# Delta rule of a hybrid layer: block turns on VectorE in place of transfers through memory, decay masks from constants by accumulating transfers, and another order of the fill products

## Chip, cores and metric

One core of one Trainium2 chip runs one layer of a diffusion backbone. The metric is the device time of the whole kernel in microseconds, as the median of several runs. TensorE (PE), VectorE (DVE), ScalarE (ACT), GpSimd (POOL) and SyncE (SP, here only a queue of transfers) each work through their instructions in order; semaphores couple them.

## The reference, cut to what matters

The layer is: half a feed-forward block, then two mixers side by side (2-D neighbourhood attention, and a gated delta rule in both directions), merged by gates, then half a feed-forward block. The change lies in the delta rule. Per head, direction and chunk of 64 tokens (shortened; the last three lines stand for the scan's step):

```python
decay = jnp.exp(jnp.where(lower, g[..., :, None] - g[..., None, :], -jnp.inf))
m = jnp.where(strict, jnp.einsum('...ik,...jk->...ij', k_beta, k) * decay, 0.0)
uw = triangular_solve(jnp.eye(GDN_CHUNK) + m, rhs, left_side=True, lower=True, unit_diagonal=True)
# then a scan over the chunks:
v_new = u - w @ s
s_next = s * g_tot + k_tail^T @ v_new
o = q_decayed @ s + (q k^T * decay) @ v_new
```

The kernel uses steps of 128 tokens, and computes the inverse of I + m once per step rather than solving. There are six steps s (two over the context, four over the 512 latent tokens), four heads and two directions.

## The kernel before

**The stage.** All of this runs in one stage, from about 718 to 967 us of the profiled span. Two streams are woven into each other on TensorE.

*Fills.* The columns of w_in that the delta rule doesn't need (q, k, v of the attention, the gates) are computed meanwhile: `fill_spill` (L784) takes one column of 128 features, rounds its weights to a high part `wh` on ScalarE (CAST, L137) and takes the remainder `wl` on VectorE (L139), does 24 products of 128x512 (eight k, each high x high, high x low, low x high, by `mm3k`, L192 to L194), copies the result out on ScalarE and stores it. It yields after each quarter, six products. `turn(kind, i)` (L1064) is called at places of the delta rule; it adds `RATE[kind][i]` to an account and issues that many quarters, tied behind the last product of the delta rule. A scheduler with its own model of time then orders the instructions of each engine; TensorE takes them in that order.

*The delta rule.* Three bases bi, each of two steps s = 2 bi and 2 bi + 1, each step of two pairs of heads p; four 128x128 matrices (two directions, two heads) lie beside each other in a tile.
- `gram` (L1114), four times per base, makes the decay tile `Dt` (a row of cumulated gates broadcast to all partitions by a transfer from `gcd`, L1118; on VectorE subtract the column's gate and add the mask, four times, L1122; an exponential of 128x512 on ScalarE, L1123), the products k k^T and q k^T on TensorE (tiles `pq`; for s = 2, 3 they are copied to `kq` tiles, written to memory `kqd`, and read back for s = 4, 5, L1093 to L1098), then `Bt` (L1128) and `At` (L1134) on VectorE. `Bt` is written to memory `bd` (L1131). For s = 2 the decay lives in half of the output accumulators `oacc`, else in tiles `Dt`.
- `base_inverse` (L1140) inverts all 32x32 diagonal blocks of a base at once, on VectorE, row by row: 31 rows of a product and a reduction (L1159, L1160), with the blocks spread over the partitions. It reads the blocks from `bd` in pieces of 128 bytes into `Ltr` and `L` (L1152), turns half of them by a ScalarE copy (L1153), sets diagonals on GpSimd (L1146 to L1155), and writes the result `Xt` to memory `rd`.
- `inverse` (L1173), twice per base, reads four pieces of it into tiles T0 and T1 (L1180, all named T in the profile), transposes 32x32 blocks on VectorE (L1182, L1183) and then builds the 128x128 inverse from the blocks by small products (tiles `pi`), with VectorE (L1202, L1218, L1229), ScalarE (L1193, L1219, L1237) and GpSimd (L1194) between them.
- `scan_step` (L1249), once per step and pair, carries the state S: products `pc`, and on VectorE r, vn, S and the outputs.

The order in which these are written, each of them calling `turn`, is:

```python
step(grams(0)); base = grams(1); turn("l", 0)
inv_of(0, 0); step(base, 4); inv_of(0, 1); step(base)
scan_of(0, 0); scan_of(0, 1); base = grams(2); scan_of(0, 2); step(base, 2); scan_of(0, 3); step(base, 2)
inv_of(1, 0); step(base, 2); scan_of(1, 0); step(base)
scan_of(1, 1); inv_of(1, 1); inv_of(2, 0); scan_of(1, 2); scan_of(1, 3); inv_of(2, 1)
# then the four scans of base 2, gdn_out, and the attention (first product sc, L1446)
```

Of the kernel before, what the change touches and what calls it, by code (L numbers as in the profile page):

```python
# [58 lines left out]
def body(ctx, tc, I, out, dbg=None):  # L59
# [1054 lines left out]
    def gram(p, s, bd, g):  # L1114
# [3 lines left out]
        nc.sync.dma_start(Dt[:], bass.AP(gcd.tensor, gcd.offset + (4 * s + 2 * p) * P, [[0, P], [24 * P, 2], [1, 2 * P]]))  # L1118
        for m, (d, c, i) in enumerate(mats):
            msk = cst[:, (C_MF if d == 0 else C_MB):][:, 0:P]  # L1120
            with tc.issue_after(marks["At" if s > 3 else "Bt"]) if s > 1 else nullcontext():
                V.scalar_tensor_tensor(Dt[:, m], Dt[:, m], gcum[:, d, s, 2 * p + i:2 * p + i + 1], msk, op0=ALU.subtract, op1=ALU.add)  # L1122
# [17 lines left out]
    def base_inverse(bd, rd):  # L1140
# [6 lines left out]
        for q in range(4):  # L1147
            G.memset(Xt[32 * q:32 * q + 32].rearrange("p c k -> p (c k)")[:, q % 2:512:34], 1.0)
        st = 32 * P + 32
        for q in range(4):  # L1150
            dst = tr[32 * q:32 * q + 32] if q < 2 else L[32 * q:32 * q + 32]
# [1 line left out]
        S.copy(L[0:64].rearrange("p r c -> p c r"), tr[:])  # L1153

        G.memset(L[:].rearrange("p r c -> p (r c)")[:, 0:1024:33], -1.0)  # L1155
        for i in range(1, 32):
# [3 lines left out]
            V.tensor_reduce(Xt[:, 0:c, i], t[:, 0:c, 0:i + 1], AX, ALU.add, negate=True)  # L1160
# [12 lines left out]
    def inverse(bi, st, rd, Bts):  # L1173


        T0 = tl(gq, [P, 8, 32], "T0", 2)
# [5 lines left out]
        V.transpose(fl(T0, 0), fl(T1, 0))  # L1182
        V.transpose(fl(T1, 4), fl(T0, 4))  # L1183
# [7 lines left out]
        for b, r in enumerate(blk):  # L1191
            o = 32 * (b % 2)
            S.copy(T6[r, :, o:o + 32], T0[r])  # L1193
# [724 lines left out]
```

## Time and profile before

| | us |
|---|---|
| median of 3 runs | 1499.81 (1499.24 to 1501.12) |
| the profiled execution | 1495.44 |
| its span, first to last instruction | 1493.7 |
| TensorE busy in it | 1434.0 (96%), granted clock 0.993 on the mean |
| VectorE, ScalarE, GpSimd busy | 1144.7, 661.9, 212.4 |
| the delta-rule stage | 718 to 967 |

Times in the profile are microseconds from the start of the span. A row of the timeline has the start, the duration, the engine, the line, the operation, the tiles out<-in, the shape, and, in brackets, how long the engine had been idle and what released it. A row of the waits has the engine, what waited, what it waited for, then the total, the number of times and the longest. A row of groups has the count, the busy time, the mean of one in ns, and the idle time before. Matmuls overlap, so their durations are longer than the steps from one to the next.

### The profile page before, as it was taken

To read this page: it belongs to the slowest core of one execution; us is meant where nothing else is said; L and a number is where in the kernel's file an instruction comes from. 1 tells how busy PE (TensorE), PEld (TensorE's weight loads), DVE (VectorE), ACT (ScalarE), POOL (GpSimd) and SP (SyncE) were. 2 spreads that over 40 slices of the span, in tenths; PEclk is the share of its full clock that TensorE was granted. 3 is DMA by queue.
4 is the path that set the end of the run, shared out by engine and by line. 5 is a ranking of instruction groups with operands and counts; after the bars stand their busy time and mean duration, and the time that the engine had idled before them with its cause. 6 is when DMAs were issued, how large, how long until landed. Compare 5 with 4: busy or idle time off the path is not lost.

```text
span 1493.7 us, 23926 instructions
## 1 busy us (share of the span) xinstructions
PE 1434.0 (96%) x9117; PEld 1258.3 (84%) x9117; DVE 1144.7 (77%) x1975; ACT 661.9 (44%) x1090; POOL 212.4 (14%) x262
## 2 busy tenths in 40 slices
PE   6999999999999999999998899999999999999997
PEld 4778989999998777888886778877778999998886
...
GB/s 372 211 257 225 222 238 187 137 174 166 170 198 404 181 178 129 84 92 88 159 222 203 167 68 125 92 276 131 100 169 149 64 129 113 85 114 134 263 98 84
DMA packets 109236, 248.56 MB, mean 166 GB/s; under 512 B 29049, under 2 KB 44481, under 8 KB 109121
## 3 DMA queue, kind: packets, MB, share of 16 engines
...
## 4 chain that ended last, share of the span: by engine, by line
PE 71%; DMA 10%; DVE 9%; ACT 4%; issue 3%; POOL 1%; SPq 1%; DVEq 0%; ACTq 0%; POOLq 0%
PE ps L211 15%; PE pm L192 5%; PE pm L193 5%; PE pm L194 5%; PE ps L533 4%; PE ps L535 4%; PE ps L534 4%; PE ps L1692 3%; PE ps L1694 3%; PE ps L1693 3%; PE ps L193 3%; PE ps L192 3%; PE ps L194 3%; PE pc L1049 3%; DMA wr<-in_up_dram 2%
## 5 line engine op out<-in xcount | busy, mean ns | idle before, releaser
L139 DVE TENSOR_TENSOR wl<-wr,wh 128x1024 fp32r<-128x1024 f32 (+1 forms) x184 | 226.0, 1233 | 112.9 <-ACT wh L137 111.3
L137 ACT CAST wh<-wr 128x1024 fp32r<-128x1024 f32 (+1 forms) x184 | 185.6, 1013 | 278.5 <-PE pm L193 72.7
L192 PE MATMUL pm<-uxh,wh 128*128 128x512 f32 x320 | 131.6, 411 | 0.0
L194 PE MATMUL pm<-uxh,wl 128*128 128x512 f32 x320 | 126.3, 395 | 0.8 <-DVE wl L139 0.8
L193 PE MATMUL pm<-uxl,wh 128*128 128x512 f32 x320 | 126.5, 395 | 0.0
L211 PE MATMUL ps<-wh,hx 128*128 128x512 f32 x352 | 96.1, 391 | 0.1
L211 PEld LDWEIGHTS ps<-wh,hx 128*128 128x128 f32 x352 | 65.9, 188 | 14.5 <-ACT wh L137 0.5
L280 DVE SCALAR_TENSOR_TENSOR adap<-wr,crow 128x1024 f32<-128x1024 f32 x61 | 74.3, 1218 | 2.4 <-DMA wr<-in_w_adaT_dram 1.7
L192 PE MATMUL ps<-uh,wh 128*128 128x256 f32 (+1 forms) x208 | 69.2, 334 | 3.8 <-ACT wh L137 3.8
L194 PEld LDWEIGHTS pm<-uxh,wl 128*128 128x128 f32 x320 | 60.6, 190 | 13.8 <-DVE wl L139 0.9
L192 PEld LDWEIGHTS pm<-uxh,wh 128*128 128x128 f32 x320 | 60.8, 190 | 11.1 <-ACT spill L796 0.2
L193 PEld LDWEIGHTS pm<-uxl,wh 128*128 128x128 f32 x320 | 60.9, 190 | 10.3
L114 POOL TENSOR_TENSOR rs<-ve,mhalf 128x1 f32<-128x1 f32 (+2 forms) x46 | 49.0, 1066 | 140.6 <-DVE ve L110 138.2
L193 PE MATMUL ps<-ul,wh 128*128 128x256 f32 (+1 forms) x208 | 67.9, 327 | 0.0
L194 PE MATMUL ps<-uh,wl 128*128 128x256 f32 (+1 forms) x208 | 67.0, 328 | 0.0
L193 PE MATMUL ps<-uxl,wh 128*128 128x256 f32 (+1 forms) x192 | 60.5, 318 | 2.2 <-DVE uxl L139 2.2
L192 PE MATMUL ps<-uxh,wh 128*128 128x256 f32 (+1 forms) x192 | 59.8, 318 | 1.6 <-ACT uxh L137 1.4
L194 PE MATMUL ps<-uxh,wl 128*128 128x256 f32 (+1 forms) x192 | 60.1, 316 | 0.0
L137 ACT CAST wh<-ra 128x1024 fp32r<-128x1024 f32 x31 | 32.6, 1052 | 59.7 <-PE ps L534 20.2
L533 PE MATMUL ps<-ur,wh 128*128 128x384 f32 x168 | 56.5, 336 | 0.0
L534 PE MATMUL ps<-ur,wh 128*128 128x384 f32 x168 | 56.4, 336 | 0.0
L533 PE MATMUL ps<-uh,wh 128*128 128x384 f32 x168 | 56.4, 336 | 0.0
...
## 6 DMA issues: line engine op xcount, KB each, us to landing
...
```

Of the source, the lines that this page charges most:

```text
L114: G.tensor_tensor(rs[:], ve[:], mhalf[:, 0:n], ALU.pow)
L137: S.copy(hi, src)
L139: marks["lo"] = V.tensor_tensor(lo, src, hi.bitcast(F32), ALU.subtract).ins
L192: T.matmul(ps, a, uh[:, k, :], start=(k == 0), stop=False)
L193: T.matmul(ps, a, ul[:, k, :], start=False, stop=False)
L194: marks["mm"] = T.matmul(ps, b, uh[:, k, :], start=False, stop=(k == nk - 1)).ins
L211: T.matmul(banks[t][d][:, c0:c1], a[:, sl], b[:, d * 512 + c0:d * 512 + c1], start=first and j == 0, stop=last and j == 2)
L280: V.scalar_tensor_tensor(pr[:], raw[:], 1.0, crow, op0=ALU.mult, op1=ALU.mult, accum_out=col[:, c:c + 1])
L533: T.matmul(ps[:], a, mh, start=k == 0, stop=False)
L534: T.matmul(ps[:], a, ml, start=False, stop=False)
L535: T.matmul(ps[:], b, mh, start=False, stop=k == 3)
L1049: last[0] = T.matmul(*a, **k).ins
```

## The change

It does six things.
1. The order of the 24 products of a fill: first, for each k, high x high and high x low (16 products), then all eight with the low part of the weights. They stand on one line now (L790).
2. Other numbers in `RATE`.
3. The decay tiles of s > 1: a constant mask `msk` is brought by a transfer on SP, the row of gates is added to it by an accumulating transfer that GpSimd issues, and ScalarE takes four exponentials of 128x128 with the column's negated gate (`ngc`) as the bias. The VectorE operations of L1122 and the single exponential stay for s < 2 alone. For s = 3 the tile is one of the `r` tiles.
4. The diagonal blocks of `Bt` are copied by ScalarE into a compact tile `W`, four copies per `gram` (`blocks`), and turned into `L` by two transpositions on VectorE, the second of 1024 columns with a strided source; `bd`, `Ltr` and their transfers go. The diagonal is set on VectorE.
5. The start values of `Xt` come from a constant `xt0` by a transfer.
6. `Xt` is turned to `Z` on VectorE, copied to T0 and T1 by four ScalarE copies, and transposed as before; `rd` and its transfers go. `inverse` takes the finished tiles.

```diff
         px = tl(pm, [P, NX], *PMB)
-        for k in range(KT):
-            if k and k % (KT // parts) == 0:
+        prods = [(w[0], u, k) for k in range(KT) for u in (uxh, uxl)] + [(w[1], uxh, k) for k in range(KT)]
+        for n, (a, u, k) in enumerate(prods):
+            if n and n % (3 * KT // parts) == 0:
                 yield
-            mm3k(px[:], w[0], w[1], uxh, uxl, k)
+            marks["mm"] = T.matmul(px[:], a[:, k * P:k * P + P], u[:, k, :], start=n == 0, stop=n == 3 * KT - 1).ins
...
-    RATE = {"g": (2, 3.0, 0.7), "l": (7.2,), "i": (1.5, 0, 0), "s": (0.7, 0.9, 0.5)}
+    RATE = {"g": (2, 2.4, 0.6), "l": (2,), "i": (1.2, 0.2, 0.7), "s": (0.6, 0.8, 0.9)}
...
+    ngc = tl(gq, [P, 2, 6, 4], "ngc")
+    S.activation(ngc[:], gcum[:], AF.Copy, scale=-1.0)
...
+        if s == 3:
+            return tl(gq, [P, 4, P], "r", 2)[:]
         return tl(gb_, [P, 4, P], "Dt", 2)[:]
...
+    def blocks(W, Bt, p, st):
+
+        m0 = 4 * st + p
+        for b in range(4):
+            r = slice(32 * b, 32 * b + 32)
+            marks["W"] = S.copy(W[r, 8:24].rearrange("p (d m) c -> p d m c", d=2)[:, :, m0:m0 + 3:2], Bt[r, :, r].rearrange("p (d i) c -> p d i c", d=2)).ins
+
+    def gram(p, s, W):
...
+        row = bass.AP(gcd.tensor, gcd.offset + (4 * s + 2 * p) * P, [[0, P], [24 * P, 2], [1, 2 * P]])
+        if s > 1:
+            nc.sync.dma_start(Dt[:], I["msk"])
+            with tc.issue_after(marks["Tt"]) if s > 4 else nullcontext():
+                G.dma_start(Dt[:], row, accum_op=ALU.add)
+        else:
+            nc.sync.dma_start(Dt[:], row)
         for m, (d, c, i) in enumerate(mats):
-            msk = cst[:, (C_MF if d == 0 else C_MB):][:, 0:P]
-            with tc.issue_after(marks["At" if s > 3 else "Bt"]) if s > 1 else nullcontext():
+            if s > 1:
+                with tc.issue_after(marks["Ti" if s > 4 else "Wg"]):
+                    S.activation(Dt[:, m], Dt[:, m], AF.Exp, bias=ngc[:, d, s, 2 * p + i:2 * p + i + 1])
+            else:
+                msk = cst[:, (C_MF if d == 0 else C_MB):][:, 0:P]
                 V.scalar_tensor_tensor(Dt[:, m], Dt[:, m], gcum[:, d, s, 2 * p + i:2 * p + i + 1], msk, op0=ALU.subtract, op1=ALU.add)
-        S.activation(Dt[:], Dt[:], AF.Exp)
+        if s < 2:
+            S.activation(Dt[:], Dt[:], AF.Exp)
...
-                nc.sync.dma_start(bass.AP(bd.tensor, bd.offset + g * MSTR, [[P, P], [4 * MSTR, 4], [1, P]]), Bt[:])
+                blocks(W, Bt, p, s % 2)
...
-        tr = tl(gb_, [64, 32, 32], "Ltr")
-        Xt = tl(gb_, [P, 16, 32], "Xt", 2)
-        G.memset(Xt[:], 0.0)
...
-            nc.sync.dma_start(dst, bass.AP(bd.tensor, bd.offset + (q // 2) * 8 * MSTR, [[st, 32], [P, 32], [1, 32]]))
-        S.copy(L[0:64].rearrange("p r c -> p c r"), tr[:])
-
-        G.memset(L[:].rearrange("p r c -> p (r c)")[:, 0:1024:33], -1.0)
+        with tc.issue_after(marks["Z"]) if "Z" in marks else nullcontext():
+            V.transpose(W[:, 0:8].rearrange("p m c -> p (m c)"), W[:, 16:24].rearrange("p m c -> p (m c)"))
+        V.transpose(L[:].rearrange("p r c -> p (r c)"), W[:, 0:16].rearrange("p m c -> p c m")[:, :, None].to_broadcast([P, 32, 2, 16]))
+        V.memset(L[:].rearrange("p r c -> p (r c)")[:, 0:1024:33], -1.0)
...
-        nc.sync.dma_start(bass.AP(rd.tensor, rd.offset, [[512, P], [1, 512]]), Xt[:].rearrange("p c k -> p (c k)"))
+        Z = tl(gb_, [P, 16, 32], "bt")
+        marks["Z"] = V.transpose(Z[:].rearrange("p c k -> p (c k)"), Xt[:].rearrange("p c k -> p (c k)")).ins
+        z = Z[:].rearrange("p c (q m) -> p m (c q)", q=2)
+        fl = lambda t, m: t[:, m:m + 4].rearrange("p m c -> p (m c)")
+        for st in range(2):
+            T0 = tl(gq, [P, 8, 32], "T0", 2)
+            T1 = tl(gq, [P, 8, 32], "T1", 2)
+            S.copy(T0[:, 0:4], z[:, 4 * st + 8:4 * st + 12])
+            S.copy(T1[:, 4:8], z[:, 4 * st:4 * st + 4])
+            V.transpose(fl(T1, 0), fl(T0, 0))
+            V.transpose(fl(T0, 4), fl(T1, 4))
+            turned.append((T0, T1))
         yield
...
-    def inverse(bi, st, rd, Bts):
-
-
-        T0 = tl(gq, [P, 8, 32], "T0", 2)
-        T1 = tl(gq, [P, 8, 32], "T1", 2)
-        for dst, d in ((T1, 0), (T0, 1)):
-            for q in range(2):
-                nc.sync.dma_start(dst[q:P:2, 4 * d:4 * d + 4], bass.AP(rd.tensor, rd.offset + (2 * d + q) * 16384 + st * 2048, [[32, 64], [2 * 2048, 4], [1, 32]]))
...
+    def inverse(bi, st, Bts):
+
+        T0, T1 = turned.pop(0)
...
+        marks["Wg"] = marks.get("W")
+        W = tl(gb_, [P, 24, 32], "W")
+        Xt = tl(gb_, [P, 16, 32], "Xt", 2)
+        nc.sync.dma_start(Xt[:].rearrange("p c k -> p (c k)"), I["xt0"])
...
+    a["xt0"] = _start()
+    a["msk"] = np.repeat(a["cst"][:, C_MF:C_MF + 2 * P].reshape(P, 2, 1, P), 2, 2).reshape(P, 4, P)
```

The change moves instructions on the engines; three places.

TensorE around the first product of base 2's first inverse (`pi<-T,Bt`). Before, the scan's products (`pc`) stand among fill products (`pm`):

```order
4350 L193 MATMUL pm_9053<-uxl_4691,wh_8979 128x512
4351 L194 MATMUL pm_9053<-uxh_4690,wl_8980 128x512
4352 L1049 MATMUL pc_9083<-vn_9076,ktail_9078 128x128 x4
4353 L1049 MATMUL pc_9093<-S_1619_8724,qT_5227 128x128
4354 L1049 MATMUL pc_9093<-S_1619_8724,qT_5228 128x128
4355 L1049 MATMUL pc_9093<-S_1619_8724,qT_5227 128x128
4356 L1049 MATMUL pc_9093<-S_1619_8724,qT_5228 128x128
4357 L192 MATMUL pm_9053<-uxh_4690,wh_8979 128x512
4358 L1049 MATMUL pi_8870<-T_1632_8854,Bt_8139 32x32 x4
4359 L1049 MATMUL pi_8870<-T_1632_8854,Bt_8166 32x32 x4
4360 L1049 MATMUL pi_8870<-T_1632_8854,Bt_8139 32x32 x4
4361 L1049 MATMUL pi_8870<-T_1632_8854,Bt_8166 32x32 x4
```

After, the lines of TensorE ahead of that inverse:

```order
4080 L1051 MATMUL pc_8943<-vn_8910,At_7453 128x128 x4
4081 L1051 MATMUL pc_8963<-S_1603_8626,kT_5223 128x128
4082 L1051 MATMUL pc_8963<-S_1603_8626,kT_5224 128x128
4083 L1051 MATMUL pc_8963<-S_1603_8626,kT_5223 128x128
4084 L1051 MATMUL pc_8963<-S_1603_8626,kT_5224 128x128
4085 L1051 MATMUL pc_8979<-r_8974,Tt_1278_6937 128x128 x4
4086 L1051 MATMUL pc_8997<-vn_8990,ktail_8992 128x128 x4
4087 L1051 MATMUL pc_9007<-S_1603_8626,qT_5227 128x128
4088 L1051 MATMUL pc_9007<-S_1603_8626,qT_5228 128x128
4089 L1051 MATMUL pc_9007<-S_1603_8626,qT_5227 128x128
4090 L1051 MATMUL pc_9007<-S_1603_8626,qT_5228 128x128
4091 L1051 MATMUL pi_8766<-T_1580_8534,Bt_8034 32x32 x4
```

The fill products have left this place: from the row of the inverse before it (the last `pi<-Tt,Y`) to this one there is now no fill among the scans of steps (1, 2) and (1, 3). Counted over the stage, 515 fill products stand ahead of this inverse before, and 388 now; behind it 107 and 234. Ahead of the very first `pi` product of base 0 there were 256 and are 196, and ahead of the last `pq` product 30 fewer.

VectorE where base 0 begins. Before, the masks of the next grams and two weight remainders stand between the last `Bt` and the first row:

```order
815 L1128 SCALAR_TENSOR_TENSOR Bt_7059<-pq_7043,beta_5207,oacc_1279_6940 128x128 x4
816 L1122 SCALAR_TENSOR_TENSOR oacc_1278_6939<-oacc_1278_6939,gcum_5208,cst_5205 128x128 x4
817 L1122 SCALAR_TENSOR_TENSOR oacc_1279_6940<-oacc_1279_6940,gcum_5208,cst_5205 128x128 x4
818 L1122 SCALAR_TENSOR_TENSOR Dt_7405<-Dt_7405,gcum_5208,cst_5205 128x128 x4
819 L139 TENSOR_TENSOR wl_7102<-wr_7099,wh_7101 128x1024
820 L1122 SCALAR_TENSOR_TENSOR Dt_7489<-Dt_7489,gcum_5208,cst_5205 128x128 x4
821 L139 TENSOR_TENSOR wl_7266<-wr_7263,wh_7265 128x1024
822 L1159 TENSOR_TENSOR bt_7147<-L_7133,Xt_7135 128x2
823 L1160 TENSOR_REDUCE Xt_7135<-bt_7147 128x1
```

After, in their place:

```order
815 L1149 SCALAR_TENSOR_TENSOR Bt_7071<-pq_7052,beta_5207,oacc_1280_6942 128x128 x4
816 L138 TENSOR_TENSOR wl_7117<-wr_7114,wh_7116 128x1024
817 L1165 STREAM_TRANSPOSE W_7005<-W_7005 128x256
818 L1166 STREAM_TRANSPOSE L_7148<-W_7005 128x1024
819 L1167 MEMSET L_7148 128x32
820 L1171 TENSOR_TENSOR bt_7152<-L_7148,Xt_7006 128x2
821 L1172 TENSOR_REDUCE Xt_7006<-bt_7152 128x1
```

The masks (L1122) are gone, and the transpositions of W and L and the diagonal stand ahead of the first row. One of the two weight remainders has moved into the rows (`wl_7288`, behind nine of them).

VectorE at the end of base 0. Before:

```order
896 L1159 TENSOR_TENSOR bt_7234<-L_7133,Xt_7135 128x15x31
897 L1160 TENSOR_REDUCE Xt_7135<-bt_7234 128x15
898 L1159 TENSOR_TENSOR bt_7237<-L_7133,Xt_7135 128x512
899 L1160 TENSOR_REDUCE Xt_7135<-bt_7237 128x16
900 L139 TENSOR_TENSOR wl_7572<-wr_7569,wh_7571 128x1024
901 L1122 SCALAR_TENSOR_TENSOR Dt_8159<-Dt_8159,gcum_5208,cst_5205 128x128 x4
902 L1159 TENSOR_TENSOR bt_7803<-L_7789,Xt_7791 128x2
```

After:

```order
894 L1171 TENSOR_TENSOR bt_7242<-L_7148,Xt_7006 128x512
895 L138 TENSOR_TENSOR wl_7569<-wr_7566,wh_7568 128x1024
896 L1172 TENSOR_REDUCE Xt_7006<-bt_7242 128x16
897 L1153 TENSOR_TENSOR At_8058<-kq_8055,Dt_8027 128x512
898 L1176 STREAM_TRANSPOSE bt_7245<-Xt_7006 128x512
899 L1165 STREAM_TRANSPOSE W_7259<-W_7259 128x256
900 L1166 STREAM_TRANSPOSE L_7716<-W_7259 128x1024
901 L1184 STREAM_TRANSPOSE T_1342_7248<-T_1341_7247 128x128
902 L1185 STREAM_TRANSPOSE T_1341_7247<-T_1342_7248 128x128
903 L1184 STREAM_TRANSPOSE T_1344_7254<-T_1343_7253 128x128
904 L1185 STREAM_TRANSPOSE T_1343_7253<-T_1344_7254 128x128
```

An `At` product of s = 4 on a `kq` tile read back from memory stands ahead of the transposition to Z (named `bt` here, since it takes a buffer of that tile); behind it stand the next base's W and L and the transpositions of T. On ScalarE, sixteen of the new exponentials (for the two `oacc` halves and the two `r` tiles) stand between base 0's last copies to W and the rounding `wh_7287`, whose remainder is `wl_7288`; eight more (of `Dt`) stand ahead of the last copy to a `kq` tile.

More of the change, by code (lines that the diff above doesn't have):

```diff
@@ L31 @@
 BWD_CH = (1, 0, 5, 4, 3, 2)
-MSTR = P * P + P
 C_MF = 0
@@ L1137, in gram, with base_inverse @@
         return Bt, At
-    def base_inverse(bd, rd):
+    turned = []
+    def base_inverse(W, Xt):
         L = tl(gb_, [P, 32, 32], "L")
-        tr = tl(gb_, [64, 32, 32], "Ltr")
-        Xt = tl(gb_, [P, 16, 32], "Xt", 2)
-        G.memset(Xt[:], 0.0)
[L1147 to L1151, printed above, removed]
-            nc.sync.dma_start(dst, bass.AP(bd.tensor, bd.offset + (q // 2) * 8 * MSTR, [[st, 32], [P, 32], [1, 32]]))
-        S.copy(L[0:64].rearrange("p r c -> p c r"), tr[:])
-        G.memset(L[:].rearrange("p r c -> p (r c)")[:, 0:1024:33], -1.0)
+        with tc.issue_after(marks["Z"]) if "Z" in marks else nullcontext():
+            V.transpose(W[:, 0:8].rearrange("p m c -> p (m c)"), W[:, 16:24].rearrange("p m c -> p (m c)"))
+        V.transpose(L[:].rearrange("p r c -> p (r c)"), W[:, 0:16].rearrange("p m c -> p c m")[:, :, None].to_broadcast([P, 32, 2, 16]))
+        V.memset(L[:].rearrange("p r c -> p (r c)")[:, 0:1024:33], -1.0)
         for i in range(1, 32):
@@ L1159, in base_inverse @@
             V.tensor_tensor(t[:, 0:c, 0:i + 1], L[:, i:i + 1, 0:i + 1].to_broadcast([P, c, i + 1]), Xt[:, 0:c, 0:i + 1], ALU.mult)
-            V.tensor_reduce(Xt[:, 0:c, i], t[:, 0:c, 0:i + 1], AX, ALU.add, negate=True)
+            marks[("row", i)] = V.tensor_reduce(Xt[:, 0:c, i], t[:, 0:c, 0:i + 1], AX, ALU.add, negate=True).ins
             if i % 4 == 0:
                 yield
-        nc.sync.dma_start(bass.AP(rd.tensor, rd.offset, [[512, P], [1, 512]]), Xt[:].rearrange("p c k -> p (c k)"))
+        Z = tl(gb_, [P, 16, 32], "bt")
[10 more added lines that the diff above has]
+            turned.append((T0, T1))
         yield
@@ L1193, in inverse @@
             S.copy(T6[r, :, o:o + 32], T0[r])
-            G.tensor_copy(Tt[r, :, 32 * b:32 * b + 32], T1[r])
+            marks["Tt"] = G.tensor_copy(Tt[r, :, 32 * b:32 * b + 32], T1[r]).ins
         py = tl(pgq, [P, 4, 32], "pi", 2)
@@ L1236, in inverse @@
         for b in range(2):
-            S.activation(Tt[hb[1 - b], sysm(b), hb[b]], p1[hb[1 - b]], AF.Copy, scale=-1.0)
+            marks["Ti"] = S.activation(Tt[hb[1 - b], sysm(b), hb[b]], p1[hb[1 - b]], AF.Copy, scale=-1.0).ins
         return [[Tt[:, 4 * d + 2 * i + p] for d in range(2) for i in range(2)] for p in range(2)]
@@ L1324, in body @@
     Sst = [None, None]
-    res, rds, inv = {}, {}, {}
+    res, inv = {}, {}
     def grams(bi):
-        bd = tl(dp, [16 * MSTR], f"bd{bi}")[:]
-        rds[bi] = tl(dp, [64, 1024], f"rd{bi}")[:]
+        marks["Wg"] = marks.get("W")
+        W = tl(gb_, [P, 24, 32], "W")
+        Xt = tl(gb_, [P, 16, 32], "Xt", 2)
+        nc.sync.dma_start(Xt[:].rearrange("p c k -> p (c k)"), I["xt0"])
         for j in (0, 2, 1, 3) if bi == 0 else range(4):
-            res[(bi, j)] = gram(j % 2, 2 * bi + j // 2, bd, 2 * (j % 2) + j // 2)
-        return base_inverse(bd, rds[bi])
+            res[(bi, j)] = gram(j % 2, 2 * bi + j // 2, W)
+        return base_inverse(W, Xt)
     def step(gen, n=8):
@@ L1338, in inv_of @@
     def inv_of(bi, st):
-        inv[(bi, 2 * st)], inv[(bi, 2 * st + 1)] = inverse(bi, st, rds[bi], [res[(bi, 2 * st + p)][0] for p in range(2)])
+        inv[(bi, 2 * st)], inv[(bi, 2 * st + 1)] = inverse(bi, st, [res[(bi, 2 * st + p)][0] for p in range(2)])
     def scan_of(bi, j):
@@ L1833, in _consts, with _start @@
     return c
+def _start():
+    t = np.zeros((P, 16, 32), np.float32)
+    for q in range(2):
+        for c in range(16):
+            t[np.arange(P) % 32 // 16 == q, c, 2 * c + q] = 1.0
+    return t.reshape(P, 512)
 def _rope():
```

9 lines of the change are left out of this document (1 added, 8 removed).

## The prediction

> **What bounds the kernel now.** I read the page first, then the stage that the change touches, from 718 us to the first attention product, by windows of 20 us and as a whole, then what TensorE waits for there, then the places in the timelines of TensorE and VectorE. The page's row of engines, and three windows (length, then busy time and instructions of PE, PEld, DVE, ACT and POOL, the granted clock, the DMA share, GB/s):
>
> ```profile
> PE 1434.0 (96%) x9117; PEld 1258.3 (84%) x9117; DVE 1144.7 (77%) x1975; ACT 661.9 (44%) x1090; POOL 212.4 (14%) x262
> ```
> ```profile
> 820.00:840.00 20.00, 16.65 (x170) 13.72 (x169) 16.83 (x42) 7.34 (x17) 0.00 (x0) 1.00 0.60 198
> 718.00:967.00 249.00, 231.67 (x1938) 194.65 (x1936) 186.41 (x492) 102.69 (x200) 36.30 (x69) 0.99 0.50 151
> 913.50:967.00 53.50, 50.21 (x534) 43.11 (x533) 31.00 (x68) 18.16 (x41) 14.26 (x21) 1.00 0.23 76
> ```
>
> TensorE is idle for 249.00 - 231.67 = 17.3 us of the stage, 14.0 of them ahead of 913.5 and 3.3 behind. That is all an edit here can win while TensorE's own work stays. What it waits for, in the stage and in its last part:
>
> ```profile
> PE pi L1049 <- DVE Y L1229: 5.1, 3, 2.4
> PE pi L1049 <- DMA T<-rd: 4.3, 1, 4.3
> PE pi L1049 <- DVE T L1218: 1.6, 2, 1.0
> PE pq L1049 <- DVE Xt L1160: 0.9, 1, 0.9
> PE pm L194 <- DVE wl L139: 0.8, 1, 0.8
> ```
>
> Only 4.3 us wait for a transfer by name; most of the rest waits for VectorE, busy 16.83 of 20 us at 820. TensorE's fill products follow each other every 0.2265 us (a mean over undisturbed stretches; the first two rows below are such a pair), and the engine stands still until the first product on the inverses:
>
> ```profile
> 797.05 0.39 PE L193 MATMUL pm<-uxl,wh 128*128 128x512 f32 x1
> 797.28 0.39 PE L194 MATMUL pm<-uxh,wl 128*128 128x512 f32 x1
> 802.00 0.92 PE L1049 MATMUL pi<-T,Bt 32*32 32x32 f32 x32 [4.33 <-DMA T<-rd]
> 913.49 0.45 PE L1049 MATMUL pi<-T,Bt 32*32 32x32 f32 x32
> 966.99 0.39 PE L1446 MATMUL sc<-kah,qah 64*128 64x256 f32 x2
> ```
>
> On VectorE the places are the end of base 0's products, the first row of its inverse, its last row, and the last row of base 2:
>
> ```profile
> 743.55 2.18 DVE L1122 SCALAR_TENSOR_TENSOR oacc<-oacc,gcum,cst 128x128 f32<-128x128 f32 x8
> 755.99 0.16 DVE L1159 TENSOR_TENSOR bt<-L,Xt 128x2 f32<-128x2 f32 x1 [5.03 <-POOL L L1155]
> 790.12 0.69 DVE L1160 TENSOR_REDUCE Xt<-bt 128x16 f32<-128x512 f32 x1
> 900.62 0.68 DVE L1160 TENSOR_REDUCE Xt<-bt 128x16 f32<-128x512 f32 x1
> ```
>
> **The change, part by part.** The whole transport of the blocks goes. From 743.55 to 756.0 the rows of base 0 now wait 12.4 us for it. The durations for the new steps, from the stage's groups:
>
> ```profile
> L1122 DVE SCALAR_TENSOR_TENSOR Dt<-Dt,gcum,cst 128x128 f32<-128x128 f32 x32 | 10.0, 377 | 7.8 <-DMA Dt<-gcd 7.8
> L139 DVE TENSOR_TENSOR wl<-wr,wh 128x1024 fp32r<-128x1024 f32 x27 | 33.0, 1222 | 3.5 <-ACT wh L137 2.0 <-PE pi L1049 1.5
> L1182 DVE STREAM_TRANSPOSE T<-T 128x128 f32<-128x128 f32 x6 | 1.8, 303 | 3.5 <-DMA T<-rd 3.5
> L1153 ACT COPY L<-Ltr 64x1024 f32<-64x1024 f32 x3 | 6.3, 2111 | 3.3 <-DMA Ltr<-bd 3.3
> L1193 ACT COPY T<-T 32x256 f32<-32x256 f32 x24 | 9.7, 402 | 8.3 <-issue 4.3 <-DVE T L1182 3.2 <-DMA T<-rd 0.6
> L1219 ACT ACTIVATE Tt<-pi 32x128 f32<-32x128 f32 x24 | 6.4, 268 | 4.8 <-PE pi L1049 4.5
> ```
>
> In its place: the last two sets of W copies on ScalarE behind a weight rounding, about 2.7 us (eight pieces at 0.268, the nearest row, 2.1, and what is queued); the turn of W, 0.4; the turn of L, 1024 columns with a strided source, bounded by 1.22 (a contiguous pass of 1024 on VectorE) and 2.11 (ScalarE's strided copy), taken at 1.7. So base 0 starts at 743.55 + 2.7 + 0.4 + 1.7 = 748.4, 7.6 us earlier. All 48 W copies cost ScalarE 48 x 0.268 = 12.9 us against 6.3 for the copies removed; it is busy 102.69 of 249, so I cost the total at nothing, but not its queue (below).
>
> These 7.6 us aren't the gain. VectorE does rows, products, scans and weight remainders one after another from there to base 2's end, now 145.3 us, in which it waits:
>
> ```profile
> DVE Dt L1122 <- DMA Dt<-gcd: 7.0, 2, 3.9
> DVE bt L1159 <- POOL L L1155: 6.4, 2, 5.0
> DVE T L1182 <- DMA T<-rd: 2.1, 2, 1.7
> DVE At L1134 <- DMA kq<-kqd: 1.8, 2, 1.1
> DVE T L1183 <- DMA T<-rd: 1.6, 1, 1.6
> DVE vn L1269 <- PE pc L1049: 1.5, 2, 1.2
> ```
>
> Those inside the stretch (5.0 of the L wait lies ahead of it) come to 7.0 + 1.4 + 2.1 + 1.8 + 1.6 + 1.5 and four small ones of 2.5: 17.9, so work and issue take 127.4. The masks removed give back 16 of 32 in this stretch (the others lie ahead), at 0.28 from start to start (8 took 2.18) 4.5 us; three weight remainders move behind the stretch, 3 x 1.22 = 3.7. Against that, eight more scan operations fall into it, 8 x 0.28 = 2.2, and the turns: L twice 3.4, W twice 0.8, Z three times (512 columns, between 0.30 and 1.22, taken at 0.6) 1.8, memsets 0.4. Sum 127.4 - 8.2 + 8.6 = about 128: VectorE's work here stays the same. What goes is waiting: the masks' 7.0, the block tile's 1.4, the T transfers' 3.7; 5.8 stay. Base 2 ends at 748.4 + 128 + 5.8 = 882.2, and its T is ready after Z, two copies of 0.40 and two turns of 0.30 at 884.2, against 913.5.
>
> TensorE can't follow. In the order it has 388 fill products ahead of that inverse instead of 515 and 234 behind it instead of 107. Without any wait it would be there at 913.5 - 14.0 - 127 x 0.2265 = 870.7, so it waits some 13.5 us for VectorE, about the 14.0 of now, in other places: at the first pi product (60 fills fewer ahead: TensorE there at 797.67 - 13.6 - 1.7 = 782.4; T at 748.4, plus the rows' 34.8 us of now, an At product of 0.6 and 3 for Z, W, L and T, 786.8: 4.4 us, as large as now), and in the scan products that stand without any fill ahead of base 2's inverse. From 884.2 the rest is now's 53.5 plus 127 x 0.2265 = 28.8, 966.5, less the waits of the tail, now 3.3, of which I let 2.7 go because twice the fills stand there. The stage ends at 963.8 instead of 967.0: **3.2 us** less. The reordered fill products are the same 24 per column; they hide the low part's arrival, 0.8 us of wait above, in those waits already.
>
> The clock. Now two windows show a lower granted clock:
>
> ```profile
> 802.00:806.00 4.00, 3.94 (x70) 2.73 (x70) 2.40 (x12) 2.18 (x5) 1.57 (x4) 0.57 0.70 168
> 866.00:870.00 4.00, 1.78 (x35) 1.28 (x33) 3.81 (x16) 1.71 (x5) 0.49 (x2) 1.00 0.00 0
> 870.00:874.00 4.00, 3.53 (x50) 3.16 (x46) 2.71 (x9) 0.76 (x2) 0.00 (x0) 0.57 0.02 4
> ```
>
> One follows the gap of 4.33, one a window in which TensorE was busy 1.78 of 4 us in pieces. Such a window loses at most 4 x 0.43 = 1.7 us. I keep two drops, as now (the first pi product and the bare scan chain), so nothing in the sum. The Trainium skill ("TensorE: Matmul & The Clock Gate", Part 1) gives an idle window of about 3.4 us for the drop to half; the first row agrees, the second shows that short gaps close together do it too. By its rule the bare scan chain, with short waits only, would not drop, and the sum would be 1.7 us better, -4.9; by the row it drops there as well.
>
> Moved queues. SP loses the block, L and T transfers and gains masks and start values, all early. GpSimd loses its memsets and issues eight accumulating transfers. Times from issue to landing, for row transfers, the kq round trip and GpSimd's own accumulating transfers elsewhere in the kernel:
>
> ```profile
> Dt<-gcd SPq DMA_DIRECT2D x8, 256.0 KB, 5.6
> kqd<-kq SPq DMA_DIRECT2D x8, 256.0 KB, 4.1
> kq<-kqd SPq DMA_DIRECT2D x16, 128.0 KB, 3.3
> L590 POOL DMA_DIRECT2D accd<-hx x6: 531/531/597, 207.1 to 243.3; - x6
> DMA to landing us min/median/max: 2.9/4.5/8.8
> ```
>
> **Rivals.** *More than the waits named go* (A). If the remaining 5.8 us of VectorE's waits vanish too, because its partner TensorE has fewer fills ahead of each scan product, T of base 2 is ready at 878.4 and the stage ends at 958.0, 9 us less: -6 to -10. For it: five waits on TensorE's products stand in that stretch. Against: these are short, and the kq waits are transfers.
>
> *The time moves into another wait, no change* (B). Ahead of base 0's turn of Z the order puts an At product on a kq tile read back from memory; its buffer is free once the last kq copy is written out. The last such product now:
>
> ```profile
> 783.00 1.05 PE L1049 MATMUL pq<-qT,kT 128*128 128x128 f32 x8
> ```
>
> With 30 fills fewer ahead it ends at 784.05 - 30 x 0.2265 - 1.7 = 775.6; ScalarE reaches the copy behind eight exponentials (8 x 0.32, estimated from 0.268) and a spill near 780, and 4.1 + 3.3 later it is 787.4, where VectorE is at 748.4 + 35.4 = 783.8: 3.6 us of stall, the gap at the first pi becomes 8, and the stage ends where it does now: -1 to +2.
>
> *Slower, by ScalarE's queue* (C). Sixteen exponentials stand there ahead of the rounding of the second weight column, and VectorE's remainder of that column stands nine rows into base 0. They wait for mask (landed 738.8, if issued at 733.3 where the row transfers now go, plus 5.5), then the accumulating rows, four issues of 0.53 and a landing of 4.5 to 8.8: 745 to 750. ScalarE needs the last of them at about 750. From about 752 on, each microsecond stops VectorE's rows one for one, with fills, pi products and scans behind it: landing at 758 makes 6 us, less the 3.2, and twice such (the second base has the same pattern) makes +4 to +8. The Trainium skill ("SBUF — State Buffer", the box on the "DVE blocks DMA" trap) speaks for this: descriptors of a transfer issued by GpSimd wait while VectorE holds the shared port; by it such landings come late when VectorE is busiest. The rows above (2.9 to 8.8 with VectorE at work) show a spread that may be this, but no stall past 8.8.
>
> *The change doesn't do what it says* (D): the order shows the transfers and masks gone, so this is only a slip of the scheduler elsewhere, either sign.
>
> **How the numbers follow.** The profiled execution took 1495.44 (span 1493.7), 4.4 under the median 1499.81; I carry the difference over: 1499.8 - 3.2 = 1496.6. About 0.2% (3.0 us) is what a measurement here can tell from no change, so my forecast lies at that border. Chances: forecast (-1.5 to -5.5) 0.45, of which 0.27 is over the border; A 0.18; B 0.19, of it 0.15 within and 0.04 slower; C 0.14; D 0.04 slower. Faster 0.45, same 0.33, slower 0.22. The range takes A to its end and C to its beginning: 1489.5 to 1504.0.
>
> **What would show it.** Right: base 0's first row near 748, a TensorE gap of some 4 us at the first pi product, base 2's T near 884, waits in the bare scan products, first attention product near 964. Wrong: waits of VectorE on wl or on kq (C, B) in base 0, L's turn far from 1.7, TensorE's idle in the stage well under 14 us (A), or a granted clock low in more than two windows.

## The result, and the profile after

The changed kernel is slower: 1508.87 us median of 4 runs (1504.71 to 1509.24) against 1499.53 (1498.73 to 1501.12), a ratio of 1.0055 with a 95% interval of 1.0035 to 1.0074. The forecast was 1496.6 in a range to 1504.0; sign and range were both wrong. The profiled execution took 1504.71, with a span of 1502.9, so it's the quickest of the four.

The page's row of engines, and windows of the stage (now to 976.5) and of places in it:

```profile
PE 1436.8 (96%) x9117; PEld 1257.4 (84%) x9117; DVE 1145.4 (76%) x1955; ACT 681.1 (45%) x1172; POOL 219.6 (15%) x252
```
```profile
718.00:976.50 258.50, 236.56 (x1947) 197.51 (x1945) 188.84 (x473) 122.73 (x284) 39.88 (x59) 0.97 0.42 133
756.00:760.00 4.00, 0.07 (x1) 0.00 (x0) 2.20 (x6) 3.22 (x7) 0.00 (x0) 0.91 0.42 115
760.00:764.00 4.00, 3.68 (x13) 3.32 (x14) 3.79 (x13) 3.20 (x7) 0.00 (x0) 0.50 0.84 252
764.00:768.00 4.00, 4.00 (x15) 3.17 (x14) 3.72 (x14) 1.29 (x5) 0.00 (x0) 0.73 0.71 255
796.00:800.00 4.00, 2.01 (x35) 1.68 (x36) 3.79 (x14) 2.25 (x7) 1.85 (x5) 0.61 0.53 161
800.00:804.00 4.00, 4.00 (x41) 2.83 (x40) 3.52 (x17) 0.01 (x1) 1.31 (x4) 0.54 0.01 4
896.40:976.50 80.10, 78.79 (x659) 66.37 (x658) 36.76 (x74) 30.75 (x61) 17.42 (x26) 1.00 0.29 96
```

TensorE is idle for 258.50 - 236.56 = 21.9 us of the stage, 4.6 more than before, and works 80.1 us behind base 2's first inverse instead of 53.5. Its waits, and its places:

```profile
PE pi L1051 <- DVE T L1185: 6.5, 2, 6.1
PE pq L1051 <- DVE bt L1171: 4.2, 1, 4.2
PE pc L1051 <- DVE r L1275: 3.7, 3, 2.3
```
```profile
797.99 0.65 PE L1051 MATMUL pi<-T,Bt 32*32 32x32 f32 x32 [6.07 <-DVE T L1185]
896.42 0.45 PE L1051 MATMUL pi<-T,Bt 32*32 32x32 f32 x32
976.53 0.39 PE L1463 MATMUL sc<-kah,qah 64*128 64x256 f32 x2
```

The gap at the first pi product is there, larger, and a second one of 4.2 stands ahead of it. Base 2's inverse is at 896.42 where the forecast had 884.2, and the attention begins at 976.53, not 963.8. VectorE in base 0:

```profile
748.35 1.99 DVE L1166 STREAM_TRANSPOSE L<-W 128x1024 f32<-128x1024 f32 x1
750.56 0.16 DVE L1171 TENSOR_TENSOR bt<-L,Xt 128x2 f32<-128x2 f32 x1
757.80 1.23 DVE L138 TENSOR_TENSOR wl<-wr,wh 128x1024 fp32r<-128x1024 f32 x1 [3.70 <-ACT wh L136]
791.79 0.68 DVE L1172 TENSOR_REDUCE Xt<-bt 128x16 f32<-128x512 f32 x1
793.96 0.69 DVE L1153 TENSOR_TENSOR At<-kq,Dt 128x512 f32<-128x512 f32 x1 [1.49 <-DMA kq<-kqd]
```

And ScalarE, whose wh that wl waits for, with the landing of GpSimd's accumulating transfers (in the stage):

```profile
750.81 1.28 ACT L1139 ACTIVATE oacc<-oacc,ngc 128x128 f32<-128x128 f32 x4 [1.13 <-DMA oacc<-gcd]
753.47 1.28 ACT L1139 ACTIVATE r<-r,ngc 128x128 f32<-128x128 f32 x4 [1.38 <-DMA r<-gcd]
755.56 1.28 ACT L1139 ACTIVATE r<-r,ngc 128x128 f32<-128x128 f32 x4 [0.81 <-DMA r<-gcd]
756.74 1.03 ACT L136 CAST wh<-wr 128x1024 fp32r<-128x1024 f32 x1
```
```profile
oacc<-gcd POOLq DMA_DIRECT2D x2, 256.0 KB, 8.4
r<-gcd POOLq DMA_DIRECT2D x2, 256.0 KB, 12.1
```

That is the mechanism of rival C: the r rows land last, ScalarE waits for them, wh stands behind, and VectorE stops nine rows into base 0. It suggested the first theory.

### The profile page after: what moved, and what is told of

It reads as the page before. It is cut to its first block, busy times and chain, and to the rows that moved or that the text cites. A ratio compares the mean times of both kernels' runs of the same rounds, so it can differ in the third digit from the quotient of the medians.

```text
span 1502.9 us, 23872 instructions
## 1 busy us (share of the span) xinstructions
PE 1436.8 (96%) x9117; PEld 1257.4 (84%) x9117; DVE 1145.4 (76%) x1955; ACT 681.1 (45%) x1172; POOL 219.6 (15%) x252
## 5 line engine op out<-in xcount | busy, mean ns | idle before, releaser
L790 PE MATMUL pm<-uxh,wh 128*128 128x512 f32 x224 | 94.3, 421 | 1.3 <-ACT spill L796 1.2
L790 PE MATMUL pm<-uxl,wh 128*128 128x512 f32 x224 | 89.9, 401 | 0.0
L191 PE MATMUL ps<-uh,wh 128*128 128x256 f32 (+1 forms) x208 | 68.8, 332 | 4.3 <-ACT wh L136 4.3
L790 PE MATMUL pm<-uxh,wl 128*128 128x512 f32 x224 | 59.6, 397 | 0.0
L533 PE MATMUL ps<-ul,wh 128*128 128x384 f32 x168 | 56.4, 336 | 0.0
L534 PE MATMUL ps<-ur,wl 128*128 128x384 f32 x168 | 56.3, 335 | 0.0
L534 PE MATMUL ps<-uh,wl 128*128 128x384 f32 x168 | 56.3, 336 | 0.0
L210 PE MATMUL ps<-wl,hh 128*128 128x512 f32 x176 | 55.3, 389 | 0.0
L210 PE MATMUL ps<-wh,hl 128*128 128x512 f32 x176 | 55.3, 389 | 0.0
L210 PE MATMUL ps<-wl,hx 128*128 128x512 f32 x176 | 55.2, 390 | 0.0
```

Source lines behind the costliest of these rows:

```text
L191: T.matmul(ps, a, uh[:, k, :], start=(k == 0), stop=False)
L210: T.matmul(banks[t][d][:, c0:c1], a[:, sl], b[:, d * 512 + c0:d * 512 + c1], start=first and j == 0, stop=last and j == 2)
L533: T.matmul(ps[:], a, ml, start=False, stop=False)
L534: T.matmul(ps[:], b, mh, start=False, stop=k == 3)
L790: marks["mm"] = T.matmul(px[:], a[:, k * P:k * P + P], u[:, k, :], start=n == 0, stop=n == 3 * KT - 1).ins
```

## The experiments

**Two theories.** S: ScalarE's queue, held by late rows, is the main loss. R: the new rates are; they defer 127 fill products behind base 2's first inverse, which VectorE sets. One caution holds for all: the stage's first product (pq) starts between 733.2 and 738.1 in the profiled executions, with the same 744 pm products ahead of it in every kernel, so the table counts from it. Each kernel was profiled once; where one kernel was profiled twice (f2, and again as g4) the columns differ by up to 2.1 us. The table gives base 2's first pi product from there, the fill products n that stand in the order between it and the attention's first product, the time between these two, the stage from pq to the attention, and the ratio to the kernel before, as measured beside it.

| kernel | first pq | to base 2's pi | n | from there | stage | ratio (95%) |
|---|---|---|---|---|---|---|
| before | 733.20 | 180.3 | 107 | 53.5 | 233.8 | 1 |
| changed | 734.47 | 162.0 | 234 | 80.1 | 242.1 | 1.0055 (1.0035 to 1.0074) |
| e1, r exponentials later | 738.08 | 158.4 | 234 | 80.1 | 238.5 | 1.0034 (1.0021 to 1.0047) |
| e2, transfers earlier | 737.13 | 160.1 | 234 | 80.7 | 240.8 | 1.0074 (1.0055 to 1.0094) |
| e3, old decays | 735.09 | 162.5 | 234 | 80.1 | 242.6 | 1.0073 (1.0053 to 1.0094) |
| e4, old rates | 733.76 | 162.8 | 132 | 62.0 | 224.9 | 0.9931 (0.9909 to 0.9952) |
| f1, before with new rates | 735.16 | 184.0 | 234 | 81.6 | 265.6 | 1.0173 (1.0148 to 1.0199) |
| f2, e4 and e1 | 736.15 | 157.5 | 132 | 62.0 | 219.5 | 0.9918 (0.9897 to 0.9939) |
| f3, e4 and e3 | 736.63 | 166.3 | 114 | 54.9 | 221.2 | 0.9928 (0.9909 to 0.9947) |
| f4, e4, old fill order | 736.90 | 167.1 | 126 | 61.3 | 228.4 | 0.9961 (0.9947 to 0.9974) |
| g1, old l only | 737.05 | 158.5 | 222 | 82.2 | 240.6 | 1.0036 (1.0020 to 1.0052) |
| g2, old i only | 734.73 | 159.1 | 174 | 68.8 | 227.9 | 1.0014 (1.0001 to 1.0027) |
| g3, old g and l | 733.38 | 157.7 | 192 | 79.0 | 236.6 | 1.0045 (1.0028 to 1.0063) |
| h1, turns alone | 737.21 | 171.6 | 96 | 54.0 | 225.6 | 0.9986 (0.9971 to 1.0000) |

**e1, the queue.** The mark ("kq", 2, 0, 1) is set at ScalarE's copy of that kq tile.

```diff
-                with tc.issue_after(marks["Ti" if s > 4 else "Wg"]):
+                with tc.issue_after(marks["Ti" if s > 4 else ("kq", 2, 0, 1) if s == 3 else "Wg"]):
```

> The changed kernel with one edit: the eight exponentials of the two r tiles (s = 3) are tied behind ScalarE's copy of the second kq tile of s = 2, so the rounding wh of the second weight column stands ahead of them; VectorE's order and the transfers stay. Theory S (ScalarE's queue, held by late accumulating rows, is the main loss): VectorE's wait for wl in base 0 falls from 3.7 us to about 1 (the weights themselves landed at 753.6), TensorE's gap of 4.25 at 756 falls to about 1.5 and its clock drop goes, the ratio to the kernel before falls from 1.0055 by 0.002 to 0.004. Theory R (the new rates, which leave too few fill products ahead of the inverses, are the main loss): the gap moves, the ratio stays within 0.001 of 1.0055.

VectorE's wait on wl falls to 0.34 us and TensorE's gap of 4.2 goes. But TensorE then comes to the first pi product earlier than T does; the gap there grows to 8.79:

```profile
756.35 1.23 DVE L138 TENSOR_TENSOR wl<-wr,wh 128x1024 fp32r<-128x1024 f32 x1 [0.34 <-ACT wh L136]
```
```profile
797.08 0.44 PE L1051 MATMUL pi<-T,Bt 32*32 32x32 f32 x16 [8.79 <-DVE T L1185]
896.48 0.45 PE L1051 MATMUL pi<-T,Bt 32*32 32x32 f32 x32
```

Counted from pq, base 2's inverse comes 3.6 us earlier and so does the attention. By the ratios it is 0.2% of the 0.55%, but the two intervals overlap. So S is worth some 3 us, which these runs alone don't separate from noise, and it isn't the main loss.

**e2, the transfers earlier.**

```diff
+    pre = {}
+    for s in (2, 3):
+        for p in range(2):
+            pre[(s, p)] = decay_place(s, p)
+            nc.sync.dma_start(pre[(s, p)][:], I["msk"])
+            G.dma_start(pre[(s, p)][:], bass.AP(gcd.tensor, gcd.offset + (4 * s + 2 * p) * P, [[0, P], [24 * P, 2], [1, 2 * P]]), accum_op=ALU.add)
     for _ in range(N0 * FS):
         next(fills)
```

> The changed kernel with the mask transfers and the accumulating row transfers of s = 2 and 3 issued at the head of the stage, ahead of the first fills; nothing else is edited. Theory S: these rows land by about 745 instead of 747.8 to 755.5, ScalarE no longer waits for them, VectorE's wait of 3.7 us falls under 1, the ratio falls to between 0.999 and 1.003. Theory R: ratio within 0.001 of 1.0055. If landing takes 7 to 13 us each there too, the slowness is of the queue of accumulating transfers itself and not of that stretch's load.

Inconclusive. Counted from pq the first row transfer was issued 4.1 us earlier (739.08 - 737.13 against 740.49 - 734.47) and the four landed 2.4 to 3.8 us earlier, 9 to 13.5 us after their issue. VectorE's wait on wl fell to 1.7, not under 1, base 2's inverse came 1.9 us earlier, no more than two executions of one kernel can differ, and the ratio, 1.0074, is in neither theory's range and can't be told from the changed kernel's.

**e3, the decay part undone** (all rows by SP, masks on VectorE, one exponential of 512).

```diff
-        if s > 1:
-            nc.sync.dma_start(Dt[:], I["msk"])
+        if s > 9:
+            nc.sync.dma_start(Dt[:], I["msk"])
...
-            if s > 1:
+            if s > 9:
...
```

> The changed kernel with the decay part undone: all rows come by plain transfers on SP, masks and exponentials as in the kernel before (the r tile for s = 3 stays). Theory S: no stall on wl, gap at 756 gone, though VectorE gets 4.5 us more of masks in the row stretch: ratio 0.999 to 1.003. Theory R: ratio stays at 1.0055 or rises by VectorE's 4.5 us to 1.008.

S fails here: with no accumulating transfer and no stall on wl the time stays at 1.0073. TensorE's gap has only moved to the first pi product, though this edit also gives VectorE the masks back:

```profile
796.30 0.65 PE L1051 MATMUL pi<-T,Bt 32*32 32x32 f32 x32 [11.98 <-DVE T L1186]
```

**e4, the rates undone.**

```diff
-    RATE = {"g": (2, 2.4, 0.6), "l": (2,), "i": (1.2, 0.2, 0.7), "s": (0.6, 0.8, 0.9)}
+    RATE = {"g": (2, 3.0, 0.7), "l": (7.2,), "i": (1.5, 0, 0), "s": (0.7, 0.9, 0.5)}
```

> The changed kernel with the rates of before. Theory S: the stall of about 3.7 us in base 0 stays, the time moves by less than 3 us either way (ratio 1.0035 to 1.0075). Theory R: ratio falls to 1.001 or below, since fills stand ahead of the first pi product and between the scan products again.

Faster than both kernels, 1490.49 us. The stall on wl is still there (3.41 us), and base 2's inverse starts where it did. What has changed is that TensorE has fills to do: it's idle for 240.60 - 230.91 = 9.7 us of the stage, and its clock is 1.00 throughout.

```profile
756.63 1.22 DVE L138 TENSOR_TENSOR wl<-wr,wh 128x1024 fp32r<-128x1024 f32 x1 [3.41 <-ACT wh L136]
```
```profile
896.59 0.45 PE L1051 MATMUL pi<-T,Bt 32*32 32x32 f32 x32
958.62 0.39 PE L1463 MATMUL sc<-kah,qah 64*128 64x256 f32 x2
```
```profile
718.00:958.60 240.60, 230.91 (x1941) 193.27 (x1939) 189.86 (x472) 121.82 (x283) 42.03 (x59) 1.00 0.46 142
896.60:958.60 62.00, 60.51 (x597) 52.36 (x596) 36.02 (x77) 22.84 (x50) 17.33 (x23) 1.00 0.25 87
```

**f1, the new rates alone on the kernel before** (the edit of e4 in the other direction).

> The kernel before with the new rates alone. Theory R (the rates put 127 fill products behind base 2's first inverse, whose time VectorE sets; each costs 0.2265 us at the end unless that inverse comes earlier by as much): base 0's T stays near 802 and base 2's first pi near 912, TensorE's gap at the first pi grows from 4.3 to 15 to 18 us, the stage ends 24 to 28 us later, ratio 1.015 to 1.019. Rival Q (the rates hurt only together with the new block path and its queues): ratio within 0.004 of 1.

The ratio is in the range of R, and so is the difference of the medians, 26.8 us; the profiled execution, the slowest of the four, has a stage 31.8 us longer. TensorE stands for 16.7 us at base 0's first pi product, and the 127 deferred products come at the end: 81.6 us from base 2's inverse to the attention instead of 53.5, 28.1 more, where 127 x 0.2265 is 28.8. (Base 0's first pi product came 5.6 us and base 2's 3.7 us later from pq than before, which R did not have.)

```profile
PE pi L1049 <- DMA T<-rd: 17.4, 2, 16.7
PE pc L1049 <- DVE r L1260: 6.3, 3, 5.1
PE pq L1049 <- DVE Xt L1160: 3.8, 1, 3.8
```

**f2, e4 and e1 together; f3, e4 and e3; f4, e4 with the old order of the fill products.** f2 and f3 join the edits shown; f4 is

```diff
-        prods = [(w[0], u, k) for k in range(KT) for u in (uxh, uxl)] + [(w[1], uxh, k) for k in range(KT)]
-        for n, (a, u, k) in enumerate(prods):
...
+        for k in range(KT):
+            if k and k % (KT // parts) == 0:
+                yield
+            mm3k(px[:], w[0], w[1], uxh, uxl, k)
```

> The changed kernel with the old rates (measured at 0.9931) and with the exponentials of the r tiles behind the kq copy. Theory S, in what is left of it: VectorE's wait of 3.4 us on wl falls to about 1 and TensorE's gap of 2.0 at 755 goes, ratio 0.990 to 0.992. Theory R: where fill products cover TensorE such a stall costs little, ratio within 0.001 of 0.9931.

> The changed kernel with the old rates and the old decay path (masks on VectorE, plain rows, no accumulating transfers). If the new decay path carries the gain of the old-rate kernel: ratio 0.998 to 1.001. If the block turns carry it: VectorE's 4.5 us more in the row stretch are partly covered, ratio 0.993 to 0.996.

> The changed kernel with the old rates and the old order of the 24 products of a fill (low part of the weights needed by the third product). If the new order is what covers VectorE's late wl: TensorE waits some 2 to 4 us on wl in base 0, ratio 0.9945 to 0.998. If not: ratio within 0.001 of 0.9931.

f2 is the fastest version: 1486.46 us. TensorE is idle for only 237.60 - 232.87 = 4.7 us of its stage:

```profile
718.00:955.60 237.60, 232.87 (x1962) 195.77 (x1960) 191.06 (x473) 123.62 (x287) 43.59 (x60) 1.00 0.47 144
```

Its ratio is in the range of what is left of S, and VectorE's longest wait on wl in base 0 is down to 0.5; but the intervals of e4 and f2 overlap. f3 is as fast as e4: the new decay path, without the edit of e1, gives nothing that can be measured once the rates are right.

f4 loses 0.3% against e4. The size is what its expectation gave for an order that covers late weight remainders; the sign is not there. TensorE's weight loads wait 0.5 us for a wl in this stage, not 2 to 4. Its longest wait is for ScalarE's copy of a finished fill, which stands behind the exponentials of the late r rows (2.02 us in e4):

```profile
762.26 0.50 PE L191 MATMUL pm<-uxh,wh 128*128 128x512 f32 x1 [3.82 <-ACT spill L797]
```

TensorE's idle time in the stage is the same in both, 9.6 and 9.7 us, while the granted clock, 1.00 throughout in e4, was 0.62 from 762 to 766 and 0.57 from 855 to 859 in f4. What the new order covers stays open.

**g1 to g3, the rates one by one; g4, f2 again.** The old values of l, of i, and of g and l:

```diff
-    RATE = {"g": (2, 2.4, 0.6), "l": (2,), "i": (1.2, 0.2, 0.7), "s": (0.6, 0.8, 0.9)}
+    RATE = {"g": (2, 2.4, 0.6), "l": (7.2,), "i": (1.2, 0.2, 0.7), "s": (0.6, 0.8, 0.9)}
...
+    RATE = {"g": (2, 2.4, 0.6), "l": (2,), "i": (1.5, 0, 0), "s": (0.6, 0.8, 0.9)}
...
+    RATE = {"g": (2, 3.0, 0.7), "l": (7.2,), "i": (1.2, 0.2, 0.7), "s": (0.6, 0.8, 0.9)}
```

> The changed kernel with only the rate l back at 7.2. In its order 36 more fill products stand ahead of base 2's first inverse than in the changed kernel. Rule R (that inverse starts near 896.5 whatever the rates; each fill product ahead of it is 0.2265 us less behind it, until TensorE no longer waits): 8.2 us less than the changed kernel, ratio 0.999 to 1.002. Rival (one entry of the rates, l or i, makes the whole loss): this one gives 0.993 like the old rates, or stays at 1.0055.

> The changed kernel with only the rates i back at (1.5, 0, 0). Also 36 more fill products ahead of base 2's first inverse, but none more ahead of base 0's. Rule R: as for l alone, ratio 0.999 to 1.002, with the wait at base 0's first pi product unchanged (it shows that what counts is the sum ahead of base 2's inverse, not that wait). Rival: 1.0055 or 0.993.

> The changed kernel with the rates g and l as before, i and s new. 66 more fill products ahead of base 2's first inverse: rule R gives 14.9 us less, ratio 0.994 to 0.997, between l alone and all old rates (102 more, measured 0.9931, where TensorE's waits are nearly used up).

> The kernel with the old rates and the r exponentials behind the kq copy once more (measured 0.9918), now beside these: 0.990 to 0.9935, the fastest of the four.

g4 repeats f2: 0.9907 (0.9888 to 0.9926), 1485.09 us, with 159.6, 132, 62.0 and 221.6 in the columns of the table. g2's ratio came as expected. g1's and g3's did not: 1.0036 and 1.0045 where 0.999 to 1.002 and 0.994 to 0.997 were expected. Half of rule R stands: base 2's inverse starts 157.5 to 163 us from pq in every kernel with the new decays and fill order, whatever the rates. The other half was counted wrongly. For the stage's end what matters isn't the number ahead of that inverse but the number n between it and the attention, and the rates also change how many stand in the stage at all: 600 from pq to the attention in the other kernels, 624 in g1 and g3 and 576 in g2. So n is 222 in g1, not 198, 192 in g3, not 168, and 174 in g2, not 198. From the kernel before, the time behind is 53.5 - 107 x 0.2265 = 29.3, plus 0.2265 n: 68.7 for g2 (measured 68.8), 82.3 for the changed kernel (80.1) and f1 (81.6), 59.2 for e4 (62.0), 79.6 for g1 (82.2), 57.8 for f4 (61.3), 51.0 for h1 below (54.0), 72.8 for g3 (79.0). g3 is farthest off; TensorE waits there 4.8 us for the output accumulators just ahead of the attention, and in several places of it:

```profile
PE pc L1054 <- DVE oacc L1330: 5.5, 2, 4.8
PE pt L1446 <- ACT pT L1480: 1.8, 2, 1.6
PE pt L1478 <- ACT pr L1471: 1.6, 1, 1.6
PE sc L1463 <- ACT pr L1471: 1.2, 1, 1.2
```

What the stage gains or loses by these 24 products the attention gets or gives. Windows from the attention's first product to the span's end, in the changed kernel and in g2:

```profile
976.53:1502.90 526.37, 505.07 (x3429) 443.29 (x3428) 382.12 (x545) 228.87 (x391) 110.24 (x97) 0.99 0.41 137
962.60:1498.30 535.70, 510.89 (x3453) 448.25 (x3452) 384.28 (x546) 229.37 (x393) 107.32 (x97) 0.99 0.40 135
```

g2's stage is 14.2 us shorter than the changed kernel's, but the part behind it is 9.3 longer, 24 x 0.2265 = 5.4 for the products and 3.5 of idle time. So its ratio agreed in part by luck. In g1 and g3 that part is not shorter though 24 products have left it (527.0 and 531.0 us); TensorE is idle there for 2.9 and 2.2 us more than in the changed kernel, which accounts for a part of it, and the rest stays open.

**h1, the turns alone on the kernel before, and h2, the fill order alone.** h1 joins the edits of e3, e4 and f4, which leaves the turns of the blocks and rows (with the start values from a constant); h2 puts the new order of the 24 products into the kernel before, the edit of f4 in the other direction.

> The kernel before with the block and row turns alone (old rates, old decay path, old order of the fill products). If the turns carry the gain by themselves: 0.993 to 0.996, TensorE's gap of 4.3 at base 0's first pi product gone. If they need the new fill order, which measured about 0.003 with the old rates: 0.996 to 0.999. Above 0.999 the gain would lie in the order or the decays together, not in the turns.

> The kernel before with the new order of the 24 products of a fill alone. If the order only covers late weight remainders, of which the kernel before shows 0.8 us: ratio 0.998 to 1.000. If it is worth 0.003 by itself, as the difference between the old-rate kernels suggests: 0.996 to 0.998.

h1 measured 0.9986, h2 0.9988 (0.9974 to 1.0003): neither alone is worth more than 0.2%, but both together with the old rates (f3) gave 0.9928. The turns bring base 2's inverse 8.7 us forward from pq (171.6 against 180.3), with the new fill order 14.0 (166.3). Why the two need each other wasn't tried further. One thing that differs is the clock: in f3's stage it is 1.00 throughout, while in h1 it fell just behind base 2's first pi product, after a window in which TensorE was busy 1.59 of 4 us with no single gap over 1.80:

```profile
912.00:916.00 4.00, 1.59 (x84) 1.40 (x70) 2.45 (x9) 2.44 (x9) 1.74 (x2) 1.00 0.58 197
916.00:920.00 4.00, 3.20 (x96) 2.78 (x94) 0.71 (x2) 1.38 (x4) 0.00 (x0) 0.55 0.01 4
```

h1's profiled stage is 8.2 us shorter than before's while its median is 3.1 better; the execution's part behind the attention's start was 3.7 longer (two executions of one kernel, f2 and g4, differ by 2.7 there), and that stays open.

## Why the prediction was wrong

*What bounds it* held: what an edit could win was TensorE's 17.3 us of idle time, and the best version wins it down to 4.7.

*The step that failed* is the one from VectorE's stretch to the stage's end: "Base 2 ends at 748.4 + 128 + 5.8 = 882.2, and its T is ready ... at 884.2". It took the stretch's waits as what was left over from the waits of before. That inverse came at 896.42, from pq 162.0 instead of 151.0 (884.2 less the 733.2 of before): 11 us mis-sized. In the sum's own terms, 5.8 us of VectorE's waits were to stay between base 0's first row and base 2's last, and 12.1 were measured there (750.56 to 893.65); work and issue came to 131.0 where 128 was taken. The largest of these waits:

```profile
DVE wl L138 <- ACT wh L136: 3.7, 1, 3.7
DVE At L1153 <- DMA kq<-kqd: 2.5, 2, 1.5
DVE At L1153 <- ACT kq L1095: 1.8, 2, 1.3
```

Nearly all of the 11 us lies in base 0. From its first pi to base 2's it was 98.4 us, forecast 884.2 - 786.8 = 97.4; from pq to its first pi it was 63.5, forecast 53.6. Of these 9.9 us, 3.7 are the stall on wl (rival C), 1.5 the kq read (rival B, which gave 3.6), 0.9 the later first row, and 2.2 are short waits of VectorE that the trace puts down to ScalarE's kq copies; 1.6 stay unassigned. The exponentials were long over by then. Two of the three copies had waited for TensorE's pq products instead, which were late behind the gap of 4.25 us and the lower clock after it:

```profile
769.29 0.59 ACT L1095 COPY kq<-pq 128x512 f32<-128x512 f32 x1 [0.35 <-PE pq L1051]
769.90 0.69 DVE L1153 TENSOR_TENSOR At<-pq,oacc 128x512 f32<-128x512 f32 x1 [1.27 <-ACT kq L1095]
772.94 0.59 ACT L1095 COPY kq<-pq 128x512 f32<-128x512 f32 x1 [1.71 <-PE pq L1051]
```

*The deferred fills* were priced rightly and weighed wrongly. The sum had 28.8 us of fills behind base 2's inverse against 29.3 us by which it would come earlier, a balance of two large numbers, of which one rests on a measured step and the other on the waits of VectorE that were to go. With 18.3 us earlier (from pq, 180.3 to 162.0) and 26.6 later (80.1 against 53.5), the stage is 8.3 longer (9.3 for the whole kernel by the medians); that is the result. No rival said it: that the rates are the loss and the rest of the change a gain. f1 and e4 show it from both sides: the rates cost 1.7% on the kernel before, and without them the change gives 0.7%.

*The first pi gap* was named (4.4, measured 6.07), as a wait like the one of before; it was the sign that TensorE ran out of fills. e1 and e3 show what mending VectorE's stall on wl is worth in that case: the gap ahead goes, and the gap at the first pi grows, to 8.79 and 11.98.

*Terms:* L's turn 1.99 (taken 1.7, inside its bounds), Z's 0.70 (0.6), a W copy 0.296 (0.268). The 1.7 us that the sums for the first pi product and for rival B take off beside the fills are not explained there (two waits of its list, 0.9 and 0.8, add up to it); TensorE came to the first pi product at 791.9, not 782.4.

*The clock:* two drops were kept, one for the bare scan chain. There were two in the changed kernel's stage, behind the gaps of 4.25 and 6.07, but each was longer than one of before: by the windows from 760 and from 796 shown with the result they lost up to (0.50 + 0.27) x 4 = 3.1 and (0.39 + 0.46) x 4 = 3.4 us of TensorE's time, where the prediction had 1.7 for one. In e4, f2 and f3 there was none. The scan chain, with gaps of 0.5 to 0.9 us between 884 and 896, caused none; TensorE was busy 16.12 of 20 us there:

```profile
880.00:900.00 20.00, 16.12 (x155) 14.09 (x153) 17.53 (x44) 7.58 (x21) 3.33 (x9) 1.00 0.36 126
```

The idle window of about 3.4 us that the Trainium skill gives ("TensorE: Matmul & The Clock Gate", Part 1) fits the two drops here, whose gaps were longer. By itself it doesn't cover h1, whose clock fell with no gap over 1.80, as it did in the prediction's row at 866 (busy 1.78 of 4). So short gaps close together can bring a drop, as the prediction read it; this chain was far busier.

*Rival C* was the right mechanism at its place, with its threshold (about 752; the r rows landed at 753.5 and 755.5), but not at its price. By e1 the stall costs some 0.2% (3 us), while C's +4 to +8 was meant for the whole change; that the measured +8 to +9 is near the upper end is luck, since most of it is the rates. C's bounds for the transfers were too low: each took 7.4 to 12.7 us to land, not 4.5 to 8.8.
